# SwiGLU entry of an encoder block: weight sums of four column blocks made in DRAM, token sums read from the transposes' banks

## The chip, the cores and the metric

The kernel runs on one core of one Trainium2 chip. The core has TensorE (PE: matmuls; PEld: its weight loads), VectorE (DVE), ScalarE (ACT), GpSimd (POOL) and SyncE (SP), and 16 DMA engines. The time is device microseconds of one execution. Before the change it is 971.36 us, the median of three runs (970.71 to 972.44).

## The reference

One residual layer of a hybrid encoder runs over 16 learned meta tokens and 512 tokens of width 1024, in float32:

```
xn   = rmsnorm(h)
proj = xn @ w_in                       # stick-breaking q|k|v, differential q|k|v
y_sb = stick_breaking_attention(...) @ w_br_sb      # 8 heads
y_df = differential_attention(...)   @ w_br_df      # 8 heads
h    = h + (sigmoid gates(xn) * (y_sb, y_df), summed) @ w_out
hn   = rmsnorm(h)
h    = h + (silu(hn @ w_ffn_gate) * (hn @ w_ffn_up)) @ w_ffn_down   # d_ff = 2816
out  = rmsnorm(h), meta tokens dropped
```

The change lies in the two products `hn @ w_ffn_gate` and `hn @ w_ffn_up`, the first half of the SwiGLU.

## The kernel before

**Precision.** Each float32 operand is split into a high and a low part (`split`, L77 and L78: ACT copies the high part, DVE subtracts it), and each product is three matmuls (`mm3`, L262 to L264). Split weights live in the tiles wh and wl, four buffers each, of which one holds 128 output columns by all 1024 inputs (eight k-tiles of 128x128).

**Stages.** The attention heads come first (eight stick-breaking, "sb", then eight differential, "df"), then the gates, the output projection (`accumulate`, L264 and its neighbours), the SwiGLU's first half over 22 blocks of 128 columns (f = 0 to 21), and its second half, the "down" product.

**Seven products for eight.** The SwiGLU's first half is a two by two block product: the left side is A11, A12 (gate weights, inputs 0 to 511 and 512 to 1023) and A21, A22 (up weights, the same halves); the right side is B11, B12, B21, B22 (the halves of the inputs by the tokens 0 to 255 and 256 to 511). For each f from 1 on it is done in seven products by Winograd's scheme. Its weight sums are S1 = A21 + A22, S2 = S1 + A11, S3 = A11 + A21, S4 = S2 + A12, with the signs of this kernel, and its token sums T1 = B11 - B12, T2 = -(T1 + B22), T3 = B22 - B12, T4 = (T1 + B22) - B21. Block f = 0 is done without it, in `early`.

- `c1` to `c4` prepare one block f. `c1` splits the gate weights. `c2` forms S1 and S2 on DVE (L208, L209) and splits them as one tile. `c3` forms S3 (L216) and splits it with A22. `c4` forms S4 (L223) and splits it. Each sum is one 128x512 addition.
- `turned(tp_)` makes the transposed tokens: for the token half `tp_` it transposes the normalised rows hn on TensorE into two PSUM tiles (L1101), takes the high part hT_h on ACT (L1106) and the low part hT_l on DVE (L1107). Then ACT copies the same banks once more as plain float32 blocks, eight 128x256 copies into the tiles bf (L1110).
- `block_sums` forms the token sums from bf on DVE, 128x1024 each (L1116, L1118, L1119, L1123), and splits the four results (L1117, L1121, L1122, L1125, recorded on L77 and L78 where `split` is used).
- In the order of the program: output projection, with `turned(0)` before its last row block, the first half of the tokens for f = 0, `c1(1)`, `turned(1)`, the products of f = 1 that need no sums, the second half of f = 0, `block_sums`, then the loop over f: `second(f)` (S2·T2, S1·T1, S3·T3), `first(f+1)` (A11·B11, A12·B21), `third(f)` (A22·T4, S4·B22). `ready` issues the preparation some steps ahead. Between these marks the instructions of each engine are ordered by the framework's scheduler, which lets later work fill the gaps of earlier work.

**Loads.** All weight loads are listed in `stream` and issued in that order on SP's queue by `stage_one` (L179), into wst, three slots of 512 KB. Only the up weights of f > 0 have slots of their own, wsu, two of them, which exist once the attention's and the merge's memory is given up.

**Background sums in DRAM.** The down product uses the same scheme with sums of weights that are made in DRAM by POOL's queue: 48 jobs (`sum_job`, L141; the DRAM tiles are recorded as ds), first 24 plain copies, then 24 accumulating DMAs (`accum_op`). One job is issued for every second unit of work inside the attention heads, each after the latest `split` then issued. In the profiled execution they run from 16 to 393 us. The same POOL queue carries the partial sums of the branches (y_sb, y_df), the copies of the keys (dk, dqk) and the gates' multiplications (L1036).

**Heads of the sb kind.** From the third head on, their k and v columns are computed by the same seven products, so there too `c2` sums a wsu tile on DVE (L208) which SP loads.

## Time and profile before

| what | value |
|---|---|
| time, median of three runs | 971.36 us |
| profiled execution: time | 970.92 us |
| profiled execution: span from the first to the last instruction | 969.1 us |
| mean granted TensorE clock | 0.998 |
| output projection ends | about 624 us |
| transposes of the second token half (L1101) | 630.2 to 636.4 us |
| last split token sum (t_l) ends | 652.3 us |
| DMA traffic | 145.83 MB, mean 150 GB/s |

Times in the views are microseconds from the start of the span. A row of the order in time gives start, duration, engine, line, operation, the tile written and those read, shapes and count; in brackets the idle time of the engine before it and what ended it. Durations of neighbouring instructions overlap at their ends, so the pace of a queue is read from start to start. A row of the chain of waits gives start, length and what the end of the kernel hung on at that moment. A row of the stretches gives the busy time of each engine with its instruction count. A row of the DMA issues gives the queue, the count, KB of one and the median microseconds from issue to landing. A few matmul records are missing from the trace.

### The profile page before, as it was taken

The numbers are of one execution on the slowest core, as the hardware profiler recorded it, in microseconds if no ns is written. First come the engines' busy times: TensorE is split into PE (matmuls) and PEld (weight loads), VectorE is DVE, ScalarE is ACT, GpSimd is POOL, SyncE is SP. The second block draws the span as 40 slices with busy tenths as digits, with TensorE's granted clock in tenths as the row PEclk, the third lists the DMA queues.
The fourth block names the chain that finished last, engine by engine and source line by source line (L and its number), as shares of the span: only waits on it lengthen the run. The fifth ranks groups of instructions, "written<-read, shape, count | busy, mean of one in ns | idle before, by whom it ended". The sixth has DMA issues, their size and how long they took to land.

```text
span 969.1 us, 16156 instructions
## 1 busy us (share of the span) xinstructions
PE 948.4 (98%) x6117; PEld 853.8 (88%) x6118; DVE 701.2 (72%) x1292; ACT 588.0 (61%) x1128; POOL 183.8 (19%) x198
## 2 busy tenths in 40 slices
PE   8998999999999999999999999989999999999997
PEld 6997888898899998999878888879999999988886
DVE  7988687766567776678632433699888888989785
ACT  7666766666566666666773433575555555666554
POOL 3201111222353433422315430000000000000013
PEclk9999999999999999999999999999999999999999
DMA  8334656679989989754739733124433334276552
GB/s 242 109 104 126 188 167 176 171 164 208 194 183 189 172 199 198 155 139 111 153 100 259 237 121 100 57 62 134 129 89 111 108 95 123 67 240 205 181 168 87
DMA packets 151439, 145.83 MB, mean 150 GB/s; under 512 B 6049, under 2 KB 116802, under 8 KB 151362
## 3 DMA queue, kind: packets, MB, share of 16 engines
q1 hardware_dynamic: 131794, 97.94, 34.0%
q0 software_dynamic: 19408, 46.80, 23.8%
q8 instruction: 48, 0.79, 0.3%
q14 instruction: 29, 0.24, 0.1%
q10 hardware_dynamic: 160, 0.07, 0.0%
HBM read 121.59 MB, written 41.94 MB: 169 GB/s over the span
## 4 chain that ended last, share of the span: by engine, by line
PE 86%; DVE 6%; ACT 4%; DMA 3%; issue 1%; DVEq 0%; ACTq 0%; SPq 0%
PE mm L264 19%; PE mm L263 19%; PE mm L262 19%; PE z L262 7%; PE z L263 7%; PE z L264 7%; DMA wst<-in_w_in_dram 2%; PE z L673 1%; PE z L672 1%; DVE wl L78 1%; PE tr L528 1%; PE z L528 1%; ACT wh L77 1%; PE tr L504 1%; PE z L556 0%
## 5 line engine op out<-in xcount | busy, mean ns | idle before, releaser
L262 PE MATMUL mm<-xT_h,wh 128*128 128x264 f32 (+2 forms) x656 | 214.3, 327 | 0.5 <-ACT xT_h L865 0.5
L78 DVE TENSOR_TENSOR wl<-wst,wh 128x1024 fp32r<-128x1024 f32 (+1 forms) x146 | 162.3, 1116 | 72.1 <-ACT wh L77 72.0
L263 PE MATMUL mm<-xT_l,wh 128*128 128x264 f32 (+2 forms) x656 | 213.2, 325 | 0.5
L264 PE MATMUL mm<-xT_h,wl 128*128 128x264 f32 (+2 forms) x656 | 212.8, 324 | 0.0
L77 ACT CAST wh<-wst 128x1024 fp32r<-128x1024 f32 (+1 forms) x146 | 140.2, 962 | 103.0 <-PE mm L263 70.0
L263 PEld LDWEIGHTS mm<-xT_l,wh 128*128 128x128 f32 x656 | 123.4, 188 | 10.4 <-DVE xT_l L866 1.3
L262 PEld LDWEIGHTS mm<-xT_h,wh 128*128 128x128 f32 x656 | 123.6, 188 | 10.0 <-ACT xT_h L865 0.9
L264 PEld LDWEIGHTS mm<-xT_h,wl 128*128 128x128 f32 x656 | 123.4, 188 | 9.9
L263 PE MATMUL mm<-hT_l,wh 128*128 128x256 f32 x284 | 80.6, 285 | 0.7 <-DVE hT_l L1107 0.7
L262 PE MATMUL mm<-hT_h,wh 128*128 128x256 f32 x284 | 80.3, 285 | 0.6 <-DVE sg L1202 0.6
L264 PE MATMUL mm<-hT_h,wl 128*128 128x256 f32 x284 | 80.1, 283 | 0.0
L1322 POOL TENSOR_TENSOR outs<-hres,gF 128x512 f32<-128x512 f32 x4 | 7.2, 1799 | 283.2 <-DVE hres L1308 278.1
L141 POOL DMA_DIRECT2D ds<-in_w_ffn_down_dram x36 | 28.5, 791 | 156.0 <-ACT wh L77 106.0
L676 DVE CUSTOM_DVE_ANT_0 pr<-z,bias 128x144 f32<-128x144 f32 (+3 forms) x64 | 30.9, 502 | 35.0 <-PE z L673 34.9
L263 PEld LDWEIGHTS mm<-hT_l,wh 128*128 128x128 f32 x284 | 53.7, 189 | 1.1 <-DVE hT_l L1107 1.1
L262 PEld LDWEIGHTS mm<-hT_h,wh 128*128 128x128 f32 x284 | 53.4, 189 | 1.0 <-DVE sg L1202 0.8
L264 PEld LDWEIGHTS mm<-hT_h,wl 128*128 128x128 f32 x284 | 53.6, 189 | 0.0
L262 PE MATMUL mm<-o_h,wh 128*128 128x512 f32 x128 | 53.1, 415 | 0.0
L262 PE MATMUL z<-wh,da 128*128 128x512 f32 (+1 forms) x132 | 50.9, 386 | 0.3 <-DVE hres L1308 0.3
L264 PE MATMUL mm<-o_h,wl 128*128 128x512 f32 x128 | 50.8, 397 | 0.0
L263 PE MATMUL mm<-o_l,wh 128*128 128x512 f32 x128 | 50.1, 392 | 0.3 <-DVE o_l L744 0.3
L263 PE MATMUL z<-wl,da 128*128 128x512 f32 (+1 forms) x132 | 50.4, 382 | 0.0
(344 smaller groups left out, 2560.1 us busy)
## 6 DMA issues: line engine op xcount, KB each, us to landing
wst<-in_w_in_dram SPq DMA_DIRECT2D x40, 512.0 KB, 7.2
ds<-in_w_ffn_down_dram POOLq DMA_DIRECT2D x30, 512.0 KB, 5.1
wst<-in_w_ffn_gate_dram SPq DMA_DIRECT2D x22, 512.0 KB, 3.8
wsu<-in_w_ffn_up_dram SPq DMA_DIRECT2D x21, 512.0 KB, 3.8
y_df<-y_out POOLq DMA_DIRECT2D x32, 256.0 KB, 5.7
wst<-in_w_gate_dram SPq DMA_DIRECT2D x16, 512.0 KB, 5.9
slots<-ds SPq DMA_DIRECT2D x13, 512.0 KB, 3.3
ds<-ds POOLq DMA_DIRECT2D x10, 512.0 KB, 8.1
```

Of the source, the lines that this page charges most:

```text
L77: cast["last"] = (hi_copy or nc.scalar.copy)(hi, src)
L78: (lo_eng or nc.vector).tensor_tensor(lo, src, hi.bitcast(F32), op=ALU.subtract)
L141: tc.add_manual_dep(nc.gpsimd.dma_start(dst, src, **kw).ins, cast["last"].ins.name, paced)
L262: nc.tensor.matmul(ps, lhsT=ah, rhs=bh, start=(start and i == 0), stop=False, skip_group_check=skip)
L263: nc.tensor.matmul(ps, lhsT=ah, rhs=bl, start=False, stop=False, skip_group_check=skip)
L264: nc.tensor.matmul(ps, lhsT=al, rhs=bh, start=False, stop=(stop and i == n - 1), skip_group_check=skip)
L504: nc.tensor.transpose(pt[:, j * P:(j + 1) * P], vT[:, j * P:(j + 1) * P], ident)
L528: nc.tensor.transpose(pt[:, (t - j) * P:(t - j + 1) * P], blocks(t, j * P, (j + 1) * P), ident)
L672: nc.tensor.matmul(o, lhsT=q[c][:, qs], rhs=k[c][:, 0, k0:k1], start=True, stop=False)
L673: nc.tensor.matmul(o, lhsT=q[c][:, qs], rhs=k[c][:, 1, k0:k1], start=False, stop=True)
L676: nc.vector.tensor_tensor_reduce(po, zz, bb, scale=1.0, scalar=-3.0e38, op0=ALU.add, op1=ALU.max, accum_out=mx[:, t, c:c + 1])
L1322: nc.gpsimd.tensor_tensor(outs[t][:, D1], hres[:, t, D1], gF[:, D1], op=ALU.mult)
```

## The change

For f = 1 to 4 the weight sums are no longer made on DVE. Two DRAM tiles hold them for 512 columns: s21 (S2 in k-tiles 0 to 3, S1 in 4 to 7) and s34 (S3 and S4). Sixteen more background jobs make them: eight plain copies and eight accumulating DMAs of 512 KB, put into `background` at a place written as a slice. The loads of a block become fg (gate weights, 512 KB), fb (s21, 512 KB), fc (S3 from s34 and A22 from the up weights, two DMAs of 256 KB) and fd (S4, 256 KB), all in wst; each is only split (`made_of`). From f = 5 on a block is prepared as before.

The jobs are issued by `tick`, one for every second call: at the units of the heads as before, and also at the units of the gates (f > 1), and twice per block in the SwiGLU's loop, one job for each call.

The token sums change their order: in `turned(1)`, DVE subtracts straight out of the banks, eight 128x256 operations. The first four give -T1 from B11, the other four T1 + B22 from that. The eight copies L1110 of `turned(1)` go; `block_sums` keeps two additions (T3, T4) and the four splits, of which T1's takes a scale of -1.

```
+    ff_order = [("fg", 0), ("fu", 0), ("fg", 1), ("fg", 2), ("fb", 1), ("fc", 1), ("fd", 1)]
+    for f in range(2, 5):
+        ff_order += [("fb", f), ("fc", f), ("fg", f + 1), ("fd", f)]
+    ff_order += [("fu", 5)] + [(n, f) for f in range(6, NFF) for n in ("fg", "fu")]
...
+    ff_jobs = sum_jobs(raw_ff, kept_ff, (0, 2))
+    background = sum_jobs(raw_down, lambda w, k0: w_sum[w, k0][:, 0:min(2, NK - k0)], DK)
+    background = background[:-len(DK) * 8] + ff_jobs + background[-len(DK) * 8:]
+    ticks = [0]
+
+    def tick(num=1, den=2):
+        ticks[0] += 1
+        if background and ticks[0] * num // den > (ticks[0] - 1) * num // den:
+            background.pop(0)()
...
         for k in range(KT):
-            nc.scalar.activation(bf[k // 4][tp_][:, k % 4], banks[k // 4][:, k // 2 % 2, k % 2 * 256:(k % 2 + 1) * 256],
-                                 AF.Copy, scale=g_ffn[:, k:k + 1])
+            p = banks[k // 4][:, k // 2 % 2, k % 2 * 256:(k % 2 + 1) * 256]
+            if tp_ == 0:
+                nc.scalar.activation(bf[k // 4][0][:, k % 4], p, AF.Copy, scale=g_ffn[:, k:k + 1])
+            else:
+                x, y = (bf[0][0], bf[0][1]) if k < 4 else (bf[0][1], bf[1][1])
+                nc.vector.scalar_tensor_tensor(y[:, k % 4], p, g_ffn[:, k:k + 1], x[:, k % 4], op0=ALU.mult, op1=ALU.subtract)

     def block_sums():
         (b11, b12), (b21, b22) = bf
         sub, add = ALU.subtract, ALU.add
-        nc.vector.tensor_tensor(b11, b11, b12, op=sub)
-        split(*tsum["t1"], b11)
-        nc.vector.tensor_tensor(b12, b22, b12, op=sub)
-        nc.vector.tensor_tensor(b22, b11, b22, op=add)
-        th, tl = tsum["t2"]
-        nc.scalar.activation(th, b22, AF.Copy, scale=-1.0)
-        nc.vector.scalar_tensor_tensor(tl, b22, -1.0, th.bitcast(F32), op0=ALU.mult, op1=sub)
+        for n, v in (("t1", b12), ("t2", b22)):
+            th, tl = tsum[n]
+            nc.scalar.activation(th, v, AF.Copy, scale=-1.0)
+            nc.vector.scalar_tensor_tensor(tl, v, -1.0, th.bitcast(F32), op0=ALU.mult, op1=sub)
+        nc.vector.tensor_tensor(b11, b22, b11, op=sub)
         nc.vector.tensor_tensor(b21, b22, b21, op=sub)
-        for n, v in (("t3", b12), ("t4", b21)):
+        for n, v in (("t3", b11), ("t4", b21)):
             split(*tsum[n], v)
...
+    FIRST = {c1: ("fg", ("a11", "a12")), c2: ("fb", ("s2", "s1")), c3: ("fc", ("s3", "a22")), c4: ("fd", ("s4",))}
+
+    def made_of(fn, f):
+        name, ws = FIRST[fn]
+        n = at_of[name, f]
+        stage(n + STAGE - 1)
+        generic(n)
+        wh, wl = loaded[name, f]
+        for w, k in zip(ws, (K1, K2)):
+            ops[f, w] = wh[:, k], wl[:, k]
...
             for fn, f in jobs[made["n"]:upto]:
+                if fn is not generic and f < 5:
+                    made_of(fn, f)
+                    continue
...
             ready(at_job(c4, f) + 2)
+            tick(1, 1)
+            tick(1, 1)
+        assert not background
```

More of the change, by code (lines that the diff above doesn't have):

```diff
@@ L80, in block_kernel @@
     stream = []
+    sums_dram = ctx.enter_context(tc.tile_pool(name="sums_dram", bufs=1, space=bass.MemoryType.DRAM))
     def cols(key, view, c0):
@@ L113, in block_kernel @@
             rows(("out", half, k0), w_out, half * 512, k0)
-    for f in range(NFF):
-        cols(("fg", f), w_fg, f * P)
-        cols(("fu", f), w_fu, f * P)
+    ff_sum = {n: sums_dram.tile([P, 8, 512], F32, name=f"ff_{n}") for n in ("s21", "s34")}
+    ff_order = [("fg", 0), ("fu", 0), ("fg", 1), ("fg", 2), ("fb", 1), ("fc", 1), ("fd", 1)]
+    for f in range(2, 5):
+        ff_order += [("fb", f), ("fc", f), ("fg", f + 1), ("fd", f)]
+    ff_order += [("fu", 5)] + [(n, f) for f in range(6, NFF) for n in ("fg", "fu")]
+    for n, f in ff_order:
+        if n == "fc":
+            stream.append(((n, f), [(ff_sum["s34"], (f - 1) * P, 0, 4), (w_fu, f * P, 4, 8)], 0, P, 0, KT))
+        elif n == "fd":
+            stream.append(((n, f), ff_sum["s34"], (f - 1) * P, P, 4, KT))
+        else:
+            cols((n, f), *{"fg": (w_fg, f * P), "fu": (w_fu, f * P), "fb": (ff_sum["s21"], (f - 1) * P)}[n])
     NK = NFF // 2
     DK = range(0, NK, 2)
-    sums_dram = ctx.enter_context(tc.tile_pool(name="sums_dram", bufs=1, space=bass.MemoryType.DRAM))
     w_sum = {(n, k0): sums_dram.tile([P, 2, 512], F32, name=f"d{n}_{k0}") for n in ("s1", "s2", "s3", "s4") for k0 in DK}
@@ L130, in block_kernel, with summed_in, sum_jobs @@
                 stream.append((("down", w, k0), w_sum[w, k0], 0, 512, 0, min(2, NK - k0)))
+    def summed_in(dst, src, add):
+        kw = dict(accum_op=ALU.add, max_dma_last_dim=2048) if add else {}
+        paced = mybir.DependencyInfo(mybir.DependencyClass.Sync, mybir.DependencyReason.DATA)
+        tc.add_manual_dep(nc.gpsimd.dma_start(dst, src, **kw).ins, cast["last"].ins.name, paced)
+    def sum_jobs(raw, kept, ks):
+        return [lambda to=to, of=of, k0=k0, i=i: summed_in(kept(to, k0), (raw if of[0] == "a" else kept)(of, k0), i > 3)
+                for i, (to, of) in enumerate((("s1", "a21"), ("s2", "a11"), ("s3", "a21"), ("s4", "a12"),
+                                              ("s1", "a22"), ("s3", "a11"), ("s2", "s1"), ("s4", "s2")))
+                for k0 in ks]
     def raw_down(w, k0):
@@ L134, in raw_down, with raw_ff, kept_ff @@
         return w_fd[:, k + k0:k + min(k0 + 2, NK), c0:c0 + 512]
-    def sum_job(to, of, k0, add):
-        src = raw_down(of, k0) if of in raw_at else w_sum[of, k0][:, 0:min(2, NK - k0)]
-        dst = w_sum[to, k0][:, 0:min(2, NK - k0)]
-        kw = dict(accum_op=ALU.add, max_dma_last_dim=2048) if add else {}
-        paced = mybir.DependencyInfo(mybir.DependencyClass.Sync, mybir.DependencyReason.DATA)
-        tc.add_manual_dep(nc.gpsimd.dma_start(dst, src, **kw).ins, cast["last"].ins.name, paced)
-    background = [(to, of, k0, i > 3) for i, (to, of) in enumerate(
-        (("s1", "a21"), ("s2", "a11"), ("s3", "a21"), ("s4", "a12"), ("s1", "a22"), ("s3", "a11"), ("s2", "s1"), ("s4", "s2")))
-        for k0 in DK]
+    SUM8 = {"s2": ("s21", 0), "s1": ("s21", 4), "s3": ("s34", 0), "s4": ("s34", 4)}
+    def raw_ff(w, k0):
+        v, k = {"a11": (w_fg, 0), "a12": (w_fg, 4), "a21": (w_fu, 0), "a22": (w_fu, 4)}[w]
+        return v[:, k + k0:k + k0 + 2, P:P + 512]
+    def kept_ff(w, k0):
+        n, k = SUM8[w]
+        return ff_sum[n][:, k + k0:k + k0 + 2]
+    ff_jobs = sum_jobs(raw_ff, kept_ff, (0, 2))
[6 more added lines that the diff above has]
+            background.pop(0)()
     at_of = {c[0]: n for n, c in enumerate(stream)}
@@ L177, in stage_one @@
         staged.append(st)
+        if isinstance(view, list):
+            for v, c, a, b in view:
+                nc.sync.dma_start(st[:, a:b], v[:, a:b, c:c + cw])
+            return True
         for a, b in ((0, 4), (4, 8)) if n < 2 else ((0, k1 - k0),):
@@ L992, in block_kernel @@
                     units.pop(0)()
[L993 to L995 removed]
+                    tick()
             for u in units:
```

9 lines of the change are left out of this document (4 added, 5 removed).

## The prediction

> **What bounds the kernel now.** I read first the page (span, shares of the engines, the chain that ended last), then the chain in order of time around the block that the change rewrites, then the busy time by stretch, and last the order on VectorE (DVE) there.
>
> ```profile
> span 969.1 us, 16156 instructions
> PE 948.4 (98%) x6117; PEld 853.8 (88%) x6118; DVE 701.2 (72%) x1292; ACT 588.0 (61%) x1128; POOL 183.8 (19%) x198
> ...
> PE 86%; DVE 6%; ACT 4%; DMA 3%; issue 1%; DVEq 0%; ACTq 0%; SPq 0%
> ```
>
> TensorE sets the end almost everywhere: 86% of the chain is its own work, and the change leaves every matmul in place. So a gain can only come out of the 14% where something else ends last. One such place is the entry of the SwiGLU. By stretch (columns: PE, PEld, DVE, ACT, POOL busy with instruction counts, then granted clock, DMA share, GB/s):
>
> ```profile
> 625.00:660.00 35.00, 30.64 (x238) 28.62 (x237) 32.49 (x49) 27.08 (x52) 0.59 (x1) 1.00 0.35 104
> 660.00:740.00 80.00, 80.00 (x673) 80.00 (x672) 68.78 (x108) 44.19 (x73) 0.00 (x0) 1.00 0.37 106
> ```
>
> From 660 us on the weight loads (PEld) are busy all the time and 673 matmuls pass in 80 us, 8.41 per us. In the 35 us before, PEld is busy 28.62 us, so 6.4 us are lost; by the count, 35 x 8.41 = 294 matmuls would fit and 238 ran, which is 6.7 us. Some 6.5 us is the most that this place can return. The clock is 1.00 in both, so nothing of it is throttling. DVE is busy 32.49 of the 35 us. The chain in this place, and then DVE's own order:
>
> ```profile
> 628.20 4.05 DMA wsu<-in_w_ffn_up_dram
> 632.26 0.70 DVE s L208
> 632.99 0.69 DVE s L209
> ...
> 636.45 1.14 DVE wl L78
> ...
> 638.38 0.59 DVE s L208
> ...
> 639.40 3.03 ACT bf L1110 x8
> ```
>
> ```profile
> 635.77 0.68 DVE L223 TENSOR_TENSOR wst<-s,wst 128x512 f32<-128x512 f32 x1
> 636.37 1.22 DVE L78 TENSOR_TENSOR wl<-s,wh 128x1024 fp32r<-128x1024 f32 x1
> 637.50 0.87 DVE L1107 SCALAR_TENSOR_TENSOR hT_l<-z,pcol,hT_h 128x256 fp32r<-128x256 f32 x2
> 638.29 0.68 DVE L208 TENSOR_TENSOR s<-wsu 128x512 f32<-128x512 f32 x1
> ...
> 645.35 1.22 DVE L1119 TENSOR_TENSOR bf<-bf 128x1024 f32<-128x1024 f32 x1
> 646.49 1.22 DVE L78 TENSOR_TENSOR hT_l<-bf,hT_h 128x1024 fp32r<-128x1024 f32 x1
> ...
> 651.03 1.22 DVE L78 TENSOR_TENSOR t_l<-bf,t_h 128x1024 fp32r<-128x1024 f32 x1
> ...
> 657.13 0.68 DVE L208 TENSOR_TENSOR s<-wsu 128x512 f32<-128x512 f32 x1
> ```
>
> DVE shows no idle time in these rows (a releaser in brackets would stand behind a row that follows a gap): the weight sums (L208 to L223), the low parts of the transposes (L1107), the token sums (L1116 to L1123) and the splits (L78) stand in one queue. Its pace is read from start to start, since the ends overlap: 635.77 to 636.37 is 0.60 us for a 128x512 operation, 645.35 to 646.49 is 1.14 us for a 128x1024 one, 637.50 to 638.29 is 0.79 us for two 128x256 ones out of PSUM, 0.40 each. ScalarE (ACT) adds 3.03 us in one run, the eight copies L1110, ahead of the token sums. The first SwiGLU products of these sums wait for this queue.
>
> **The change part by part.** *Weight sums off DVE.* Each row block f had four 128x512 additions (L208, L209, L216, L223). For f = 1 to 4 they go, 16 in all. Those of f = 1 and 2 stand before the last token sum: 8 x 0.60 = 4.8 us off DVE's queue. The first of f = 3 is the row at 657.13, and there TensorE is as good as full, by the row of 660 to 740: those of f = 3 and 4 are worth nothing.
>
> *Token sums from the banks.* Of the four 128x1024 additions L1116, L1118, L1119 and L1123 two go (2 x 1.14 = 2.3 us); eight 128x256 operations that read PSUM come, of the form of L1107, 8 x 0.40 = 3.2 us. DVE pays 0.9 us. ACT loses eight of the sixteen copies, the 3.03 us of the chain. The banks are now held until DVE has read them and not ACT; the one that waits for a bank is the product s1·t1, and that needs t1, which comes out of the same reads, so the hold adds no wait.
>
> The queue of DVE shortens by 4.8 - 0.9 = 3.9 us and ACT's by 3.0 us beside it; the wait for the first wsu load (its 4.05 us in the chain) goes as well, since blocks that are already summed need no wsu. I take 4.0 us as the gain: DVE has no idle time to swallow it, and 6.5 us are there to be won. What is late next is again DVE, with the splits and the third and fourth token sums. Below, if the engines' new order leaves gaps like today's, 2.0 us; above, 6.5 us.
>
> *More loads through fewer slots.* For f = 1 to 4 a block loads 512 + 512 + 512 + 256 KB instead of 2 x 512 KB, and all of it through the three wst slots on SP's queue, where wsu had two slots of its own.
>
> ```profile
> wst<-in_w_ffn_gate_dram SPq DMA_DIRECT2D x22, 512.0 KB, 3.8
> slots<-ds SPq DMA_DIRECT2D x13, 512.0 KB, 3.3
> ```
>
> A block is 84 matmuls, 84 / 8.41 = 10.0 us, so three slots give each of four loads 7.5 us. A load takes 3.8 us to land (a sum out of DRAM 3.3), and its split is two passes, DVE's of 1.14 us and one on ACT about as long: 6.1 us, 1.4 to spare. DMA traffic is 1.75 times that of a share of 0.37, about 0.65. So it costs nothing while this cover holds; each 1 us of landing beyond 5.2 us would cost at most 4/3 us per block, over four blocks. Queued behind a late slot on SP is only the next load of the same stream. fc is two transfers of 256 KB in the place of one: one more issue on an SP that is mostly idle.
>
> *Sixteen more DRAM jobs, at the head of the queue.* POOL issues them one per two units of the attention, so the rate there stays; the slice that is meant to leave some jobs in front is empty (48 jobs, and the slice drops 48), so all 16 go first and every down job comes 16 places later. Of the old list jobs 25 to 48 were accumulations; of the new one 9 to 16 and 41 to 64. By my count of the units in the loops (6 + 7 x 7 in the sb heads, 7 x 8 + 6 in the df heads, 117) 58 jobs fall in the heads and six in the gate stage; the ticks in the SwiGLU find nothing left. What a job costs others:
>
> ```profile
> 96.00:153.00 57.00, 57.00 (x374) 50.94 (x373) 42.14 (x71) 38.50 (x73) 9.63 (x16) 1.00 0.58 179
> 308.00:393.00 85.00, 85.00 (x554) 77.44 (x554) 60.27 (x159) 56.57 (x135) 33.36 (x37) 1.00 0.90 192
> 217.00:246.00 29.00, 27.78 (x183) 24.84 (x182) 18.82 (x28) 17.97 (x35) 9.45 (x11) 1.00 0.92 193
> 400.00:450.00 50.00, 50.00 (x322) 45.35 (x321) 34.57 (x97) 32.84 (x80) 14.63 (x15) 1.00 0.62 129
> ```
>
> From 308 to 393 us twelve accumulations run, from 400 to 450 none; DMA share 0.90 against 0.62, and 554 / 85 = 6.5 matmuls per us against 322 / 50 = 6.4. The ten accumulations that are new after 393 us therefore cost nothing; of the six in the gate stage, where POOL also multiplies the gates, I take the same (bounds 0 and 6 x 0.9 us, POOL's time for one by the row below). The places that do matter are two:
>
> ```profile
> 217.10 2.80 POOL L141 DMA_DIRECT2D ds<-in_w_ffn_down_dram  x3 [8.51 <-ACT kh L576]
> 308.25 0.94 POOL L141 DMA_DIRECT2D ds<-ds  x1 [2.51 <-ACT vT L515]
> 219.11 16.52 DMA wst<-in_w_in_dram
> 246.31 0.55 PE L528 MATMUL z<-ident,s 128*128 128x128 f32 x3 [1.53 <-DVE a_l L531]
> ```
>
> At 217 us three jobs start beside the first loads of the differential heads, two of them accumulations, and a load that stands in the chain takes 16.52 us; TensorE idles 1.53 us behind it. With the new list these are plain copies. Gain 0 to 1.5 us. Against it, jobs 9 to 16 (96 to 153 us) become accumulations beside the sb heads' loads:
>
> ```profile
> 108.93 0.37 SPq L179 DMA_DIRECT2D wsu<-in_w_in_dram  x1
> 137.08 0.38 SPq L179 DMA_DIRECT2D wsu<-in_w_in_dram  x1
> 142.74 0.69 DVE L208 TENSOR_TENSOR s<-wsu 128x512 f32<-128x512 f32 x1 [1.75 <-DMA wsu<-in_w_in_dram]
> 143.35 1.22 DVE L78 TENSOR_TENSOR wl<-wst,wh 128x1024 fp32r<-128x1024 f32 x1
> 144.98 0.28 PE L264 MATMUL mm<-xT_h,wl 128*128 128x264 f32 x1
> ds<-in_w_ffn_down_dram POOLq DMA_DIRECT2D x7, 512.0 KB, 4.5
> ds<-in_w_ffn_down_dram POOLq DMA_DIRECT2D x4, 512.0 KB, 8.3
> ```
>
> DVE already waits 1.75 us at the sum L208 for the wsu load issued at 137.08; behind it in DVE's queue stands the split that ends at 143.35 + 1.22 = 144.57, and TensorE takes it at 144.98. Slack 0.4 us: what such a load lands later goes on to TensorE. Two heads' loads lie among the new accumulations (108.9 and 137.1 us). The last two rows are the landing of jobs in 96 to 153 us (plain, 4.5) and in 217 to 246 us (8.3, mostly accumulations): 3.8 us more at worst, for two heads 2 x (3.8 - 0.4) = 6.8 us; at best 0. The share there is 0.58 and not 0.92 as at 217, so I take 1 us, near the lower end, and about as much won at 246 us. They cancel.
>
> The Trainium skill ("DMA: Bandwidth & Descriptors", section "Issuing engines are not separate DMA queues") speaks against this part: DMAs started from SP, ACT or POOL run on the same 16 engines and interleave, so a queue of its own protects no load from the sums. By that rule the sb heads pay, and the time would move from the forecast toward the slower rival below; the 16.52 us load agrees with it, the unchanged matmul rate from 308 to 393 us shows that it costs only where a load has no slack.
>
> Sum against the profiled execution: 969.1 us of span, 970.92 us in all; 4.0 less is 966.9. That execution lies 0.44 us under the median of the three runs, 971.36, so against the median 967.4 us.
>
> **The rivals.**
>
> *More than DVE's share returns.* ACT's copies stand in the chain beside DVE's queue, so both together may free nearly all 6.5 us, and the 1.5 us at 246 us come back: 971.4 - 8.0 = 963.4 us. For it: ACT and DVE both shorten, and the summed blocks no longer wait for wsu. Against it: splits and token sums of 1.14 us remain in line.
>
> *Nothing.* The three slots take the place of DVE: if the loads land in 6.1 us instead of 3.8, the excess over 5.2 is 0.9, times 4/3, times four blocks, 4.8 us, and the gain is eaten: 971.4 - 4.0 + 4.8 = 972.2, at half that excess 969.8. For it: the load before a wait for a slot is SP's common state. Against it: share 0.37, and sums that are complete long before they are read.
>
> *Slower, by the accumulations in the sb heads.* Above 0.4 + 4.0 / 2 = 2.4 us of added landing per load the two heads lose more than the SwiGLU wins. At the 3.8 us of the two rows: 971.4 - 4.0 + 6.8 = 974.2 us. For it: the 1.75 us wait and the slack of 0.4. Against it: share 0.58, and only two loads in the stretch.
>
> **How the numbers follow.** Forecast (965.5 to 969.2) 0.55; more returned 0.15; nothing 0.16; slower 0.14. About 0.2%, 1.9 us, is what a measurement can tell from no change. Faster: 0.55 + 0.15 and a little of "nothing", 0.71; same: 0.15; slower: the last rival, 0.14. The range takes the first two cases, "nothing" and the nearer part of the last: 963.0 to 972.3, with some 0.15 outside.
>
> **What would show it.** Right: between 625 and 660 us no L208 to L223 additions and eight fewer ACT copies, DVE's token sums ended some 4 us earlier, over 260 matmuls in the 35 us; from 660 us on still 8.4 per us with SP never the releaser of a split; in the sb heads waits on wsu up to 1 us longer; a load at 219 us well under 16.5. Wrong: new TensorE waits that end at a DMA, in blocks 2 to 5 (slots) or between 100 and 150 us (accumulations), or a first SwiGLU block that still ends 35 us after 625 with DVE idle in it.

## The result, and the profile after

The changed kernel takes 986.46 us (median of four executions, 984.68 to 987.65) against 971.18 us for the kernel before in the same measurement: a ratio of 1.0154 [1.0133, 1.0175], slower by 15 us, above the range that was predicted. The profiled execution took 985.5 us, its span 983.7 us.

To see where the time went, both traces are cut at four events that every version has: the first transposes of the last differential head (L528, after the change L561; "df head 7", counted from 0), near the end of the attention; the first transposes of the SwiGLU's tokens (L1101, now L1133), near the end of the output projection; the first and the ninth of DVE's operations `sg<-z,qx` (L1226, now L1274), one per block, of f = 1 and f = 9.

| stretch | before, us | after, us | difference |
|---|---|---|---|
| start to df head 7 | 483.68 | 484.80 | +1.1 |
| gates and output projection | 134.68 | 143.70 | +9.0 |
| entry of the SwiGLU, to f = 1 | 40.58 | 39.43 | -1.15 |
| blocks f = 1 to 9 | 79.71 | 84.69 | +5.0 |
| the rest | 230.4 | 231.1 | +0.6 |

The last two marks are instructions of DVE, and TensorE has not always done the same matmuls by then: 266 of them lie in the entry before, 268 after. The entry won little over a quarter of the 4.0 us of the forecast, and 14 us were lost in two places where the prediction had put nothing. The first lines of the page after:

```profile
span 983.7 us, 16199 instructions
PE 952.8 (97%) x6117; PEld 856.9 (87%) x6118; DVE 695.7 (71%) x1282; ACT 583.4 (59%) x1120; POOL 200.1 (20%) x214
...
PE 76%; DVE 10%; DMA 6%; ACT 4%; issue 3%; POOL 1%; SPq 0%; DVEq 0%; POOLq 0%; ACTq 0%
```

The count of matmuls is the same, 6117. DVE has ten instructions fewer and POOL sixteen more, the new jobs. TensorE's share of the chain fell from 86% to 76%; DMA's doubled from 3% to 6%. The stretches that the prediction rested on (columns as there):

```profile
625.00:660.00 35.00, 32.51 (x229) 29.21 (x228) 27.19 (x54) 24.48 (x51) 0.00 (x0) 1.00 0.29 83
660.00:740.00 80.00, 75.92 (x619) 75.12 (x618) 60.62 (x93) 42.15 (x70) 0.60 (x1) 0.98 0.47 136
96.00:153.00 57.00, 57.00 (x378) 51.12 (x377) 42.19 (x72) 39.09 (x73) 12.80 (x15) 1.00 0.80 179
400.00:450.00 50.00, 50.00 (x318) 45.15 (x317) 34.61 (x95) 33.75 (x82) 20.97 (x22) 1.00 0.99 192
```

From 660 to 740 us TensorE is no longer full, 75.92 of 80, with 619 matmuls for 673 (some of that is the later start). The two rows from the heads show the new accumulations as a higher DMA share, 0.80 for 0.58 and 0.99 for 0.62, and a TensorE that is busy throughout all the same.

**Where the gate stage lost 9 us.** After the change, POOL's queue in order of time (start, duration, operation, idle time and releaser):

```profile
504.99 0.90 POOL L144 DMA_DIRECT2D ds<-ds  x1 [24.89 <-ACT wh L77]
...
511.46 1.50 POOL L144 DMA_DIRECT2D ds<-ds  x1
512.03 4.49 POOL L801 DMA_DIRECT2D y_df<-y_out  x4
529.13 2.56 POOL L1068 TENSOR_TENSOR sg<-sg,y_df 128x512 f32<-128x512 f32 x2 [12.62 <-DMA y_df<-y_df]
531.64 0.93 POOL L144 DMA_DIRECT2D ds<-ds  x1
```

These are accumulations of the down product, which the sixteen new jobs have pushed back into this stage. Two start at 504.99 and 511.46 us, between the last partial sums of the branches (y_df<-y_out). POOL then stands 12.62 us until a branch sum has come back, and multiplies gates only at 529.13. DMA issues between 503 and 518 us (median us from issue to landing at the end of a row), after:

```profile
y_df<-y_out POOLq DMA_DIRECT2D x7, 256.0 KB, 12.6
...
ds<-ds POOLq DMA_DIRECT2D x2, 512.0 KB, 10.3
wst<-in_w_gate_dram SPq DMA_DIRECT2D x1, 512.0 KB, 17.1
y_df<-y_df SPq DMA_DIRECT2D x2, 256.0 KB, 13.3
```

and before:

```profile
y_df<-y_out POOLq DMA_DIRECT2D x5, 256.0 KB, 6.8
...
wst<-in_w_gate_dram SPq DMA_DIRECT2D x2, 512.0 KB, 6.8
y_df<-y_df SPq DMA_DIRECT2D x2, 256.0 KB, 6.2
```

A partial sum lands in 12.6 us in the place of 6.8, the load that brings it back in 13.3 for 6.2, the gate weights in 17.1 for 6.8. From there it goes on through ACT, whose instructions stand in order, to TensorE:

```profile
532.28 1.22 ACT L77 CAST mg_h<-sg 128x512 fp32r<-128x512 f32 x2 [16.03 <-DVE sg L1069]
558.56 1.04 ACT L77 CAST wh<-wst 128x1024 fp32r<-128x1024 f32 x1 [9.44 <-DMA wst<-in_w_gate_dram]
```

```profile
534.03 0.50 PE L297 MATMUL mm<-xT_h,wl 128*128 128x512 f32 x1 [2.36 <-DVE wl L78]
560.25 0.80 PE L295 MATMUL mm<-xT_h,wh 128*128 128x512 f32 x1 [4.60 <-ACT sg L808]
...
563.39 0.40 PE L296 MATMUL mm<-xT_l,wh 128*128 128x512 f32 x1
563.62 0.40 PE L297 MATMUL mm<-xT_h,wl 128*128 128x512 f32 x1
```

ACT waits 16.03 us at the split of a multiplied gate; the copies of the next weights stand behind it, and TensorE idles 2.36 us. The second gap, 4.60 us, hangs on a load of gate weights itself, in the chain of waits:

```profile
542.33 16.16 DMA wst<-in_w_gate_dram
```

It is issued between the accumulations of 541.81 and 543.55 us. After this gap seven matmuls take 3.14 us (560.25 to 563.39) where the pace of 0.23 us, from 563.39 to 563.62, would need 1.6. The granted clock (third figure from the end of a row of the stretches) is halved there, and full behind the gap of 2.36 us:

```profile
534.03:541.00 6.97, 6.96 (x31) 5.77 (x32) 3.52 (x4) 2.63 (x4) 0.99 (x2) 1.00 0.91 188
559.95:563.36 3.41, 3.12 (x7) 2.44 (x8) 1.61 (x2) 0.85 (x3) 1.72 (x1) 0.50 0.84 229
```

The losses are 2.4 + 4.6 + 1.5 = 8.5 of the 9.0 us. The Trainium skill ("TensorE: Matmul & The Clock Gate", section "Part 1: The HAM clock gate (the "warmup" mystery)") has TensorE fall to half its clock after an idle window of about 3.4 us and stay there for about as long. These two gaps agree with it; others, below, do not.

**Where the blocks lost 5 us.** Nearly all of it lies in one block: from f = 1 to f = 2 it took 14.65 us, before the change 9.75. SP's queue after the change:

```profile
639.64 1.48 SPq L212 DMA_DIRECT2D wsu<-in_w_ffn_up_dram  x2
649.03 0.53 SPq L212 DMA_DIRECT2D wst<-ff_s  x1
661.92 0.37 SPq L209 DMA_DIRECT2D wst<-ff_s  x1
662.34 0.50 SPq L209 DMA_DIRECT2D wst<-in_w_ffn_up_dram  x1
663.65 0.37 SPq L212 DMA_DIRECT2D wst<-in_w_ffn_gate_dram  x1
```

Between 649.03 and 661.92 us it issues nothing, and its waits say for what (total, times, longest):

```profile
SPq L209 <- DVE wl L78: 12.2, 1, 12.2
```

for one of DVE's splits, which gives a wst slot back. The three slots hold sums for f = 1 and 2, and those are split only around the time at which the token sums are done. Then five loads follow within 7 us, and the one that TensorE will miss is the gate weights of f = 3:

```profile
663.65 7.19 DMA wst<-in_w_ffn_gate_dram
```

```profile
670.91 1.04 ACT L77 CAST wh<-wst 128x1024 fp32r<-128x1024 f32 x1 [4.16 <-DMA wst<-in_w_ffn_gate_dram]
671.86 0.36 ACT L1258 COPY qx<-mm 128x256 f32<-128x256 f32 x1
```

```profile
669.00 0.28 PE L297 MATMUL z<-t_h,wl 128*128 128x256 f32 x1
672.28 0.39 PE L295 MATMUL mm<-hT_h,wh 128*128 128x256 f32 x1 [3.00 <-ACT qx L1258]
...
673.07 0.42 PE L296 MATMUL mm<-hT_l,wh 128*128 128x256 f32 x1
673.28 0.41 PE L297 MATMUL mm<-hT_h,wl 128*128 128x256 f32 x1
...
676.04 0.28 PE L295 MATMUL mm<-hT_h,wh 128*128 128x256 f32 x1
676.15 0.28 PE L296 MATMUL mm<-hT_l,wh 128*128 128x256 f32 x1
```

The first row is the chain of waits, then come ACT's order and TensorE's. The weights land in 7.19 us; ACT waits 4.16 us for them, and the small copy qx, for which TensorE stands, is the next in ACT's queue behind them. TensorE idles 3.00 us, and for 3.8 us afterwards matmuls follow each other every 0.21 us in the place of 0.12: another 1.7 us. Together 4.7 of the 4.9 us. The granted clock is 0.50 from 672.59 to 676.00 us. Here the stall, 3.28 us even when counted from start to start, is a little shorter than the 3.4 us of the Trainium skill, and the slow stretch is there all the same.

**Why the entry won so little.** The sums L241 of f = 5 and 6 are now the first users of the wsu slots. The slots are empty from the start, so the scheduler lets those loads (639.64 us above, twice 512 KB) and the first addition run inside the entry:

```profile
645.57 0.69 DVE L241 TENSOR_TENSOR s<-wsu 128x512 f32<-128x512 f32 x1 [1.99 <-DMA wsu<-in_w_ffn_up_dram]
```

DVE waits 1.99 us there for weights that are needed four blocks later, in the queue that was to be shortened.

### The profile page after: what moved, and what is told of

Same layout as the page of the kernel before. It is cut to its first block, busy times and chain, and to the rows that moved or that the text cites. A ratio compares the mean times of both kernels' runs of the same rounds, so it can differ in the third digit from the quotient of the medians.

```text
span 983.7 us, 16199 instructions
## 1 busy us (share of the span) xinstructions
PE 952.8 (97%) x6117; PEld 856.9 (87%) x6118; DVE 695.7 (71%) x1282; ACT 583.4 (59%) x1120; POOL 200.1 (20%) x214
## 4 chain that ended last, share of the span: by engine, by line
PE 76%; DVE 10%; DMA 6%; ACT 4%; issue 3%; POOL 1%; SPq 0%; DVEq 0%; POOLq 0%; ACTq 0%
PE mm L297 17%; PE mm L296 17%; PE mm L295 17%; PE z L295 6%; PE z L296 6%; PE z L297 6%; DVE wl L78 2%; DMA wst<-in_w_ffn_gate_dram 2%; DMA wst<-in_w_gate_dram 2%; DMA wsu<-in_w_in_dram 1%; PE z L706 1%; PE z L705 1%; DVE s L644 1%; PE tr L561 1%; DMA wsu<-in_w_ffn_up_dram 1%
## 5 line engine op out<-in xcount | busy, mean ns | idle before, releaser
L78 DVE TENSOR_TENSOR wl<-wst,wh 128x1024 fp32r<-128x1024 f32 (+1 forms) x154 | 174.2, 1135 | 75.4 <-ACT wh L77 75.0
L77 ACT CAST wh<-wst 128x1024 fp32r<-128x1024 f32 (+1 forms) x154 | 148.2, 966 | 106.1 <-PE mm L296 62.7
L296 PE MATMUL mm<-hT_l,wh 128*128 128x256 f32 x284 | 81.4, 288 | 0.3 <-DVE hT_l L1139 0.3
```

What stands on the lines that cost most here:

```text
L77: cast["last"] = (hi_copy or nc.scalar.copy)(hi, src)
L78: (lo_eng or nc.vector).tensor_tensor(lo, src, hi.bitcast(F32), op=ALU.subtract)
L296: nc.tensor.matmul(ps, lhsT=ah, rhs=bl, start=False, stop=False, skip_group_check=skip)
```

## The experiments

Each kernel was timed beside the kernel before on the same chip, whose median was 973.03 us for the first four, 972.34 for the next four, 972.57 for the three after and 972.93 for the last. The table gives the stretches of the profiled executions. The first column varies by some 2 us from execution to execution: run 6 has the attention of the kernel before. Part of that is the clock: in the profiles of runs 1, 3 and 6 TensorE runs at a granted clock of 0.50 for 3.4, 3.4 and 6.8 us between 82 and 94 us. The gates' column repeats to 0.1 us wherever at most one job falls into it. The entry holds 266 matmuls in the kernel before and in runs 2, 7, 8 and 10, 268 in the change and in run 4, 275 in run 1, 261 in runs 3, 5, 9 and 12, and 256 in runs 6 and 11. What is missing there is in the next column, at 0.12 us for one matmul.

| run | ratio to before [95%] | to df 7 | gates | entry | f = 1 to 9 | rest |
|---|---|---|---|---|---|---|
| before | 1 | 483.7 | 134.7 | 40.6 | 79.7 | 230.4 |
| after | 1.0154 [1.0133, 1.0175] | 484.8 | 143.7 | 39.4 | 84.7 | 231.1 |
| 1: after, last 16 jobs left out | 1.0053 [1.0033, 1.0072] | 485.7 | 134.7 | 39.9 | 83.9 | 231.1 |
| 2: before, jobs 32 units later | 1.0079 [1.0058, 1.0101] | 481.9 | 145.9 | 42.0 | 79.8 | 230.4 |
| 3: after, slots of their own | 1.0068 [1.0047, 1.0090] | 485.6 | 143.3 | 36.6 | 81.0 | 231.1 |
| 4: after, no early sums | 1.0117 [1.0097, 1.0136] | 483.5 | 145.3 | 37.2 | 84.2 | 230.9 |
| 5: after, own slots, jobs moved | 1.0004 [0.9995, 1.0014] | 481.5 | 134.7 | 36.6 | 83.4 | 237.7 |
| 6: before, token sums alone | 0.9996 [0.9986, 1.0005] | 485.6 | 134.7 | 37.4 | 82.4 | 231.8 |
| 7: 5 without the token sums | 1.0019 [1.0010, 1.0028] | 483.6 | 134.7 | 38.3 | 82.2 | 234.8 |
| 8: before, jobs moved as in 5 | 0.9988 [0.9977, 0.9999] | 482.2 | 134.7 | 40.5 | 83.6 | 230.4 |
| 9: after, own slots, jobs in heads | 0.9999 [0.9991, 1.0008] | 485.8 | 134.6 | 36.6 | 81.4 | 232.1 |
| 10: before, jobs in heads | 0.9968 [0.9956, 0.9980] | 481.2 | 134.6 | 40.4 | 79.7 | 230.3 |
| 11: 10 with the token sums | 0.9963 [0.9949, 0.9976] | 482.3 | 134.7 | 37.5 | 82.4 | 231.1 |
| 12: two blocks, jobs in heads | 0.9938 [0.9918, 0.9958] | 481.6 | 134.7 | 36.6 | 81.7 | 231.3 |

### The jobs in the gate stage

**1.** The last sixteen jobs are left out, so that none falls into the gate stage; a part of S2, S3 and S4 of the down product is then missing.

```diff
-    background = background[:-len(DK) * 8] + ff_jobs + background[-len(DK) * 8:]
+    background = ff_jobs + background[:32]
```

> The changed kernel without its last 16 DRAM jobs (it leaves out part of the sums S2 and S4 of the down product): 48 jobs in the same places as before the change, none after 393 us. Theory, late accumulations: the changed kernel loses 9.0 us between 504 and 629 us because its last six DRAM accumulations share the engines and POOL's queue with the accumulations of y_df and the loads that read them back; POOL, then ACT, wait in order. Then this run takes 986.5 - 9.0 = 977.5 us, the first transpose of the SwiGLU's tokens (628.66 us in the changed kernel) comes at 619.5 to 620, and the 12.6 us wait of POOL for y_df falls to some 4 us. Rival, the new places in the program (ticks in the gates, another order of instructions) cost it: 985 to 987 us. Rival, all DRAM jobs after 393 us cost evenly: part of it already gone at 485 us (484.97 in the changed kernel at the last df transposes).

Measured: 977.14 us. The gate stage takes the 134.7 us of before, and POOL's longest wait for a branch sum there is 5.8 us, not 12.62:

```profile
POOL sg L1068 <- DMA y_df<-y_df: 6.2, 2, 5.8
```

(total, times, longest). The 9 us belong to those sixteen jobs (ten in the heads, six in the gates) and to nothing else of the change; run 2 shows which.

**2.** The other way round: the kernel before, with nothing of the change but a later start of its jobs, and job issue at the gates' units as well.

```diff
-    todo, unit_count = [], [0]
+    todo, unit_count = [], [-32]
...
-                    if background and unit_count[0] % 2 == 0:
+                    if background and unit_count[0] > 0 and unit_count[0] % 2 == 0:
...
                 for u in gate(br, f, sg[br], AF.Sigmoid):
                     u()
+                    unit_count[0] += 1
+                    if background and unit_count[0] % 2 == 0:
+                        sum_job(*background.pop(0))
...
```

> The kernel before the change, with its 48 jobs started 32 units later and ticks at the units of the gates, so that its last six accumulations fall into the gate stage as in the changed kernel. Nothing else of the change is in it. Theory, late accumulations: some 9 us slower, 979 to 981 us, lost between 504 and 619 us. Rival, the cost needs the rest of the change: 970 to 972 us.

Measured: 979.88 us, and the gate stage 145.9 us, 11.2 more than before:

```profile
POOL sg L1039 <- DMA y_df<-y_df: 13.4, 1, 13.4
```

So the loss can be made in the kernel before by the place of the jobs alone. TensorE's two gaps are 3.19 and 4.01 us here, and 3.4 us at a granted clock of 0.50 stand behind each, where the change has one such stretch: that makes most of the difference between 11.2 and 9.0 us. The attention ended 1.8 us earlier, with no job in its first units, but that is within what its column varies by.

### The slots and the early sums

**3.** From f = 2 on the loads fb and fc go into the two wsu slots instead of wst. As a side effect the up weights of f = 5 and 6 are no longer the first in those slots.

```diff
-        if key[0] == "fu" and key[1]:
+        if key[0] == "fu" and key[1] or key[0] in ("fb", "fc") and key[1] > 1:
```

> The changed kernel, with the loads fb and fc of f = 2 to 4 in the two wsu slots that stand empty there. Theory, slots: the changed kernel loses 4.9 us in block f = 2 (14.65 us from the sums of f = 1 to those of f = 2, against 9.75 before), because three slots give the loads no lead, and 2 to 3 us more at the entry, because the empty wsu slots let the scheduler pull the loads and first sums of f = 5 and 6 into the entry, where DVE waits 2.0 us for them. Both go here: 986.5 - 7 = 979 to 980 us, block f = 2 in 9.8 to 10.1 us. Rival, bandwidth (the sums' loads are 1.75 times the bytes and bunch however they are placed): 985 to 987 us, a split still waits 4 us for a load. Rival, only the pulled-in sums cost: 983 to 984 us with the 4.9 us still there.

Measured: 979.18 us. The entry takes 36.64 us, 3.94 less than before: the 4.0 us of the forecast. Block f = 2 takes 10.1 us and the blocks to f = 9 lose 1.2 us in the place of 5.0. SP's queue now:

```profile
641.71 0.93 SPq L209 DMA_DIRECT2D wsu<-in_w_ffn_up_dram  x1
647.22 0.37 SPq L212 DMA_DIRECT2D wst<-in_w_ffn_gate_dram  x1
660.12 0.37 SPq L212 DMA_DIRECT2D wst<-ff_s  x1
```

TensorE's idle time in the entry falls from 4.36 us before the change to 1.53. The 3.94 us also hold five matmuls that now run behind the mark, 0.6 us, so that some 3.3 us are won, and the blocks lose 0.6 us less than the table says. The gate weights of f = 3 are asked for at 647.22 us and not at 663.65: the wait was for a slot, not for DMA. The wsu row is the up half of f = 2; there are no loads for f = 5.

**4.** The slots as in the change, but the first sum of f = 5 and 6 and their loads are tied to the latest split that stands ahead of them in the program, so that they can't be drawn into the entry.

```diff
-        nc.vector.tensor_tensor(s[:, K2], u[:, K1], u[:, K2], op=ALU.add)
+        sm = nc.vector.tensor_tensor(s[:, K2], u[:, K1], u[:, K2], op=ALU.add)
+        if f in (5, 6):
+            after_last(sm)
...
-            nc.sync.dma_start(st[:, a:b], view[:, k0 + a:k0 + b, c0:c0 + cw])
+            ld = nc.sync.dma_start(st[:, a:b], view[:, k0 + a:k0 + b, c0:c0 + cw])
+            if key in (("fu", 5), ("fu", 6)):
+                after_last(ld)
```

> The changed kernel, with the first sum and the load of the up weights of f = 5 and 6 held back behind the split that stands ahead of them in the program. Theory, slots: the entry gains 2 to 3 us (the eight token sums L1147 start that much earlier after the first transpose), block f = 2 keeps most of its 4.9 us: 983 to 985 us. Rival, only the pulled-in loads and sums cost (their 1 MB goes first and makes everything late): entry and block f = 2 both heal, 979 to 980 us.

Measured: 983.65 us. The entry takes 37.2 us, 2.2 less than with the change; block f = 2 still takes 14.7 us. The early sums cost the entry its gain, the slots cost the block behind it: two causes, told apart.

### The jobs somewhere else

**5.** Own slots, and jobs only at the even units from 15 to 96 of the heads; the remaining 23 go two per block into the SwiGLU from f = 5 on.

```diff
-        if background and ticks[0] * num // den > (ticks[0] - 1) * num // den:
+        if 14 < ticks[0] <= 96 and ticks[0] % 2 == 0:
...
-            tick(1, 1)
-            tick(1, 1)
+            for _ in range(2 if f > 4 else 0):
+                if background:
+                    background.pop(0)()
```

> The changed kernel with two repairs: the loads fb and fc of f = 2 to 4 in the wsu slots (as in the run of own slots), and the DRAM jobs between the 15th and the 96th unit of the heads (41 of them), the other 23 in the SwiGLU from f = 5 on, two per block; none beside the first sb heads' loads, none in the gates. Theory, the three costs add: late accumulations 9.1 us, slots and pulled-in sums 7.3, jobs beside the load at 82 us some 2 to 3: 986.5 - 18.5 = 968 us, 0.997 of the kernel before. Rival, the accumulations cost as much in the SwiGLU as in the gates (its own loads share the engines): 971 to 977 us, with splits or sums waiting for loads between 690 and 830 us.

Measured: 972.52 us, no difference from before. Attention, gates and entry are as good as hoped; the jobs charge in the SwiGLU instead. DVE's waits there (660 to 862 us), then the same wait in the kernel before (660 to 857 us):

```profile
DVE s L241 <- DMA wsu<-in_w_ffn_up_dram: 29.1, 16, 5.3
```

```profile
DVE s L208 <- DMA wsu<-in_w_ffn_up_dram: 10.9, 17, 1.5
```

Before, DVE waits 0.6 us on the mean for its up weights and TensorE loses nothing by it; with two accumulations per block the mean is 1.8 us, the longest 5.3, and the blocks lose 3.7 us to f = 9 and over 7 us behind it. This profile is of the slowest of the twelve executions, 975.76 us, and has 6.8 us at a granted clock of 0.50 from 776 us on; run 7, with the same jobs and no such stretch, loses 4.3 us behind f = 9.

**8.** The kernel before with its jobs placed like that (seven of them then fall into the SwiGLU), as a control.

```diff
-                    if background and unit_count[0] % 2 == 0:
+                    if background and 14 < unit_count[0] <= 96 and unit_count[0] % 2 == 0:
...
+            for _ in range(2 if f > 4 else 0):
+                if background:
+                    sum_job(*background.pop(0))
...
```

> The kernel before with its own 48 jobs moved alike (41 between the 15th and the 96th unit, 7 in the SwiGLU from f = 5 on), nothing of the change. It says what of the repaired kernel's time is the moving of jobs and not the change. Theory, the first sb heads wait 1 to 2 us for loads beside the early jobs: 969.5 us, 0.998 of before. Rival, the jobs were free where they stood: 971 us.

Measured: 971.04 us. That is the rival's time, but not for its reason: the blocks to f = 9 take 3.9 us more, 3.4 of it in the one block from f = 6 to 7, and the start gains.

**10.** The same with all 48 jobs inside the heads, at units 15 to 110, every second one.

```diff
-                    if background and unit_count[0] % 2 == 0:
+                    if background and 14 < unit_count[0] <= 110 and unit_count[0] % 2 == 0:
...
```

> The kernel before, its 48 DRAM jobs at units 15 to 110, one of every two units, instead of 2 to 96. Theory: the first head's stall behind the early jobs goes, and nothing else changes: 1.5 us under the kernel before. Rival: the stall in front only moves the wait to a later place with the same end, within 0.5 us of the kernel before.

Measured: 969.51 us, 0.9968 [0.9956, 0.9980], 3 us under the kernel before and more than the 1.5 expected. The profile shows that gain in the attention alone. TensorE idles 5.4 us in the first 95 us, 7.6 before; its wait of 0.93 us for o_l at 88.51 us is down to 0.22.

**9.** The change with own slots (those of run 3, for fb and fc from f = 2 on) and all 64 jobs in the same units, which takes two of every three.

```diff
-        if background and ticks[0] * num // den > (ticks[0] - 1) * num // den:
+        if 14 < ticks[0] <= 110 and (ticks[0] - 14) * 2 // 3 > (ticks[0] - 15) * 2 // 3:
...
-            tick(1, 1)
-            tick(1, 1)
```

> The changed kernel with the fourth-block-on loads in slots of their own, and all 64 DRAM jobs inside the attention heads: at units 15 to 110 of 117, two of every three units, none in the gate stage, none in the SwiGLU. Theory (an accumulation costs only where a load has no slack, which is the gate stage and the SwiGLU): the entry of the SwiGLU is 3.9 us shorter than before, the seventh df head starts 1 to 2 us earlier because no job runs in the first units, the gate stage takes the 114.8 us of before, the blocks f = 1 to 8 lose the 1.2 us they lost with own slots alone: 4 to 5 us under the kernel before, 0.995 to 0.996. Rival (the number of jobs per unit is what costs): at two of three units the heads' own loads are late, the seventh df head's transposes start 2 us or more after those of before, and the time is within 1 us of the kernel before or above it.

Measured: 972.27 us, the rival's case. Df head 7 comes 4.6 us later than in run 10, and 3.7 us of that lie in one stretch of the sb heads. DVE's order there, then the stretch:

```profile
176.79 0.69 DVE L241 TENSOR_TENSOR s<-wsu 128x512 f32<-128x512 f32 x1 [10.32 <-DMA wsu<-in_w_in_dram]
```

```profile
153.00:200.00 47.00, 43.30 (x274) 37.41 (x273) 31.32 (x50) 27.62 (x55) 11.23 (x13) 1.00 0.93 188
```

The wsu load issued at 162.42 us takes 14.28 us to land (5.1 us for the wsu load of this stretch in run 10), DVE stands 10.32 us at the sum, and TensorE is busy 43.30 of 47 us. Accumulating jobs were issued at 158.44 and 159.93 us, at neighbouring units, 1.5 us apart and just ahead of the load; in the change itself the four accumulations of this part came at 132.18, 135.66, 150.51 and 153.30 us. It is the mechanism of the prediction's slower rival, which cost the change nothing.

### The parts of the entry alone

**6.** The kernel before with the token sums from the banks (L1110 to L1123 as in the change), nothing else.

> The kernel before with the change of the token sums alone. Theory, DVE's queue sets the entry: 0.9 us more on DVE, 3.0 us less on ACT: within 1.5 us of the kernel before, either way. Rival, ACT's eight copies are the chain: 2 to 3 us faster, 968 to 969 us.

Measured: 971.51 us, no difference: the theory's time, but with the shorter entry of the rival. The entry is 3.2 us shorter, and the blocks behind it take 2.7 us more. Of both, 1.2 us are ten matmuls that now run behind the mark, which is neither won nor lost. TensorE's idle time falls from 4.36 to 2.31 us in the entry, and in the blocks, where it was nothing, it stands 1.18 us for a split on DVE:

```profile
PE mm L264 <- DVE wl L78: 1.2, 1, 1.2
```

The split (wl from s) starts at 658.01 us, behind the weight sums of f = 2: L209 and L216 of this block run at 655.46 and 656.58 us, where the kernel before had done them inside its long entry, at 639.67 and 640.27.

**7.** Run 5 with the token sums of before: the weight sums in DRAM alone.

> The repaired kernel (moved jobs, own slots) with the token sums of before: the weight sums alone. Theory, DVE's queue: 4.8 us off it, so this is within 1 us of the repaired kernel with both parts, 967.5 to 969 us. Rival, the token sums carry the gain: 970 us or more.

Measured: 974.64 us, 2.1 us above run 5, with intervals that overlap only between 1.0010 and 1.0014; the entry is 38.3 us, 1.6 longer than run 5's.

**11.** Run 10 with the token sums.

> The run with the 48 jobs at units 15 to 110 in the kernel before, and beside that the token sums formed from the banks; the weight sums stay on VectorE. Theory: the entry gets 3.2 us shorter, as with the token sums alone, and the weight sums on VectorE give some 2.7 us of it back in the blocks behind: 0.5 us under the run with the moved jobs alone. Rival: the 2.1 us by which the repaired kernel with the old token sums was longer is what the token sums are worth anywhere: 2 us under the run with the moved jobs alone.

Measured: 969.07 us, 0.9963 [0.9949, 0.9976] beside run 10's 0.9968 [0.9956, 0.9980]: no difference that these runs can tell. The entry is 2.8 us shorter, the blocks to f = 9 are 2.7 us longer, with the same ten matmuls and the same 1.18 us as in run 6.

### What is left of the change

**12.** DRAM sums for f = 1 and 2 only (eight jobs of 512 KB), own slots for the loads of f = 2, the token sums, and the 56 jobs at seven of thirteen units from 15 on: 55 in the heads, and the last at the first unit of the gates, at 501.8 us.

```diff
-    for f in range(2, 5):
+    for f in range(2, 3):
...
-        return v[:, k + k0:k + k0 + 2, P:P + 512]
+        return v[:, k + k0:k + k0 + 4, P:P + 256]
...
-    ff_jobs = sum_jobs(raw_ff, kept_ff, (0, 2))
+    ff_jobs = sum_jobs(raw_ff, kept_ff, (0,))
...
-        if background and ticks[0] * num // den > (ticks[0] - 1) * num // den:
+        if 14 < ticks[0] and background and (ticks[0] - 14) * 7 // 13 > (ticks[0] - 15) * 7 // 13:
...
```

> The changed kernel cut to what the runs left worth having: DRAM sums for the blocks f = 1 and 2 only (8 jobs of 512 KB in the place of 16, so 56 in all), those of f = 2 loaded through slots of their own, the sums of f = 3 and 4 on VectorE again, token sums from the banks, and the jobs at units 15 to 117, seven of every thirteen units. Theory: up to the SwiGLU it stands as the kernel before with its jobs at units 15 to 110 (df head 7 at 481.2, SwiGLU tokens at 615.8), the entry takes 36.6 us as with own slots, the blocks give back 1 us: 3 us under that kernel, 0.993 to 0.994 of the kernel before. Rival: two jobs at units beside each other, once in thirteen, still push a head's load past its sum, as at two of three units, and the sums of f = 3 and 4 give the entry's gain back: 0.997 or more, no better than the moved jobs alone.

Measured: 967.03 us, 0.9938 [0.9918, 0.9958], faster than both kernels. The entry and the stretch that failed in run 9:

```profile
616.00:653.00 37.00, 35.49 (x264) 32.50 (x263) 31.63 (x56) 28.90 (x55) 0.58 (x1) 1.00 0.36 102
```

```profile
153.00:200.00 47.00, 47.00 (x308) 41.69 (x307) 32.71 (x51) 31.76 (x61) 10.91 (x14) 1.00 0.77 170
```

TensorE is full in the sb heads again, the entry takes the 36.6 us of own slots, and the gates take 134.7 us although one accumulation falls into them. Of the 3.7 us that the entry is shorter than in run 10 the blocks to f = 9 give 2.0 back (0.6 as five matmuls behind the mark, 1.0 as TensorE's waits for qx) and the rest 1.0, so that the two profiled spans, 965.9 and 966.2 us, differ little. Run 12 is faster than the kernel before. That it also beats run 10, so that something of the change is left beside the moved jobs, is likely by the ratios, whose intervals overlap only from 0.9956 to 0.9958, and not settled.

## Why the prediction was wrong

**The step that failed first: "of the six in the gate stage, where POOL also multiplies the gates, I take the same"**, that is nothing. It measured 9.0 us (run 1 takes them away, run 2 makes 11.2 in the kernel before). The count of six jobs was right and so was the place. Wrong was the price that bounded it: 6 x 0.9 us is what POOL spends on issuing, 5.4 us at most. What the jobs charged was the landing of others. The row from 308 to 393 us, from which "nothing" was taken, is a place where loads are asked for long ahead; in the gate stage partial sums leave through POOL's queue, are added in DRAM, come back through SP's, are multiplied on POOL and split on ACT, whose queue also holds the next weights' copies. That loop had no slack for these jobs, and the prediction looked for slack only in the sb heads. The cost does not simply go by the number of jobs: the one that run 12 has there costs nothing. Its sentence on the Trainium skill ("DMA: Bandwidth & Descriptors", section "Issuing engines are not separate DMA queues") named the rule that decided: a queue of its own protects no load. In this stage the trace agrees with it, with 17.1 us against 6.8 for a load of gate weights.

**The second: the slots "cost nothing while this cover holds".** By run 3 they cost 3.7 of the 5.0 us that the blocks lost, and 4.5 us in the one block f = 1 to 2. The cover of 7.5 us per load supposed loads that are spread over a block. At the entry they are not: three slots fill with sums for f = 1 and 2 while the token sums are still being made, and stay full for 13 us. The landing of 7.19 us then came on top, with 3.0 us of idle TensorE and 1.7 us at a lower pace behind it; the estimate 0.9 x 4/3 per block had neither. The prediction's "sums that are complete long before they are read" was true and did not matter: early data are of no use without a place to put them.

**The gain of 4.0 us** was nearly the right size for what the edits can do: 3.94 us between the marks in runs 3 and 5, with own slots, of which 0.6 us are matmuls that moved behind the mark and some 3.3 us are won. That the marks give just 4.0 is luck. The change itself kept 1.15 us; run 4 shows that 2.2 us went to sums of f = 5 and 6, which the scheduler moved into the entry because their slots had become free. The prediction had not asked what the emptied wsu slots would invite. Its split of the gain was off: token sums alone shorten the entry by 3.2 us (run 6), 2.0 without the ten matmuls, and weight sums alone by some 2.1 (run 7's 38.3 against 40.4 in run 10, with as many matmuls), where it had 4.8 us for the weight sums and a cost of 0.9 on DVE for the token sums. ACT's eight copies, "3.03 us of the chain", weighed as much as DVE's additions, and the two parts overlap: 2.0 + 2.1 is more than the 3.3 that both give together. And the gain does not all stay: TensorE then waits 0.4 us (run 3) to 1.2 us (run 6) in the blocks to f = 9, where it waited for nothing before. "DVE has no idle time to swallow it" held inside the entry and not behind it.

**The accumulations in the sb heads** were to cost about 1 us and to be cancelled at 246 us. Neither came. The wait at the second sum doubled,

```profile
146.52 0.69 DVE L241 TENSOR_TENSOR s<-wsu 128x512 f32<-128x512 f32 x1 [3.94 <-DMA wsu<-in_w_in_dram]
```

but TensorE did not notice. The slack of 0.4 us was a misreading: the matmul at 144.98 us does not use the split that ends at 144.57. In the change the same matmul runs at 146.27 us, before that split starts at 147.13. What stands next in DVE's queue in the kernel before is

```profile
147.92 0.43 DVE L419 TENSOR_TENSOR vT<-mm,qq 128x264 f32<-128x264 f32 x1 [3.35 <-ACT e L606]
```

with 3.35 us of idle time ahead of it, and the later sum only ate into that. At 246 us the wait for a_l went from 1.53 to 1.35 us, 0.2 us and not 1. Here the prediction read the chain wrongly: the two loads issued there landed in 11.3 us instead of 17.6, as it expected, and TensorE's wait hardly depends on them, for in run 6, with the old list and loads of 16.5 us, it is 1.36 us. What does cost time in the attention is the first jobs: at the matmul behind o_l in one of the first sb heads, the kernel before and the change both wait,

```profile
88.51 0.39 PE L262 MATMUL z<-kh,qh 128*128 128x264 f32 x1 [0.93 <-DVE o_l L625]
```

```profile
89.79 0.39 PE L295 MATMUL z<-kh,qh 128*128 128x264 f32 x1 [2.04 <-DVE o_l L658]
```

and all eight runs without jobs before the 15th unit (2, 5 and 7 to 12) pass it at 86.0 to 87.0 us. The 1.1 us between these two rows are no more than executions differ by: runs 1, 3 and 4, with the first jobs of the change, pass it at 89.1, 88.9 and 88.4 us. In the first 95 us TensorE idles 5.4 to 5.8 us in those eight runs, and 6.5 to 8.8 us in the six others.

**The signs that the prediction named** did point at the place: "new TensorE waits that end at a DMA, in blocks 2 to 5 (slots)" came, in block 2, by way of ACT's queue; the waits between 100 and 150 us did not; and the gate stage was not on the list. The two losses were independent, 9.0 and 5.0 us, and none of the rivals had the larger one.

What stays open: which of the six jobs in the gate stage made the loss, and whether a spacing exists that costs nothing with all 64. Of the 1.2 to 2.7 us that the blocks behind the shorter entry lose in runs 3, 6, 9, 11 and 12, 0.2 to 0.5 us are left unexplained when the moved matmuls and TensorE's waits are taken off.

## What to carry to other kernels

Price a background transfer by what it does to the landing of the transfers beside it, stage by stage, and look for the stage in which data go out and come back through a chain of in-order queues; a stage that hid a dozen of them says nothing about another. When loads are moved into fewer slots, ask when each slot is given back at the moment at which its consumer is still blocked, and not at the mean rate. When a change empties a slot or a queue, ask what the scheduler will put into it. When two versions are compared between marks, count the matmuls between the marks as well: a shorter stretch may only hold less work.

## What the runs showed of the hardware

Two accumulating DMAs from DRAM to DRAM of 512 KB beside a load on another queue went with two to three times its landing time: 17.1 us for 6.8 in the gate stage, and 14.28 us for a wsu load in run 9, where it is 5.1 in run 10. It is not so wherever two come close together: in the change pairs at 132.18 and 135.66 us and at 150.51 and 153.30 us went with a median of 6.2 us for the two wsu loads from 96 to 153 us, and of 5.0 before.

A stall of TensorE can cost more than its idle time, by half the granted clock behind it: 4.60 us of idle time were followed by 3.41 us at 0.50, 1.5 us lost, and 3.00 us by 3.41 us at 0.50, 1.7 us lost. The length of one gap does not decide it. The same 3.41 us followed gaps of 2.53 us (run 3, at 535.00 us) and 2.17 us (run 8, at 716.99 us), and 6.83 us began within 1.2 us of the end of a gap of 1.73 us (run 6, at 81.03 us), but nothing followed 2.36 us in the change.
